# The first two column blocks of an output projection, computed as a pair

## The chip, the cores and the metric

The kernel runs on one core of a Trainium2 chip. Its engines work side by side: TensorE (PE in the profile, with PEld for the loads of stationary operands), VectorE (DVE), ScalarE (ACT), GpSimd (POOL) and SyncE (SP). The last two mostly issue DMA transfers here. The metric is device time in microseconds (us) of one execution, as the median of several runs.

## What is computed

One layer of a decoder trunk, on 256 rows of 2048 columns, in float32:

```python
def hybrid_layer(x, g_mix, w_in, q_gain, k_gain, w_branch, w_out, g_ffn, w_gu, w_down, rel_bias):
    h = rmsnorm(x, g_mix)
    proj = h @ w_in
...
    merged = (gates[:, :, 0] * (flat(o_a) @ w_branch[:ea])
              + gates[:, :, 1] * (flat(o_b) @ w_branch[ea:eb])
              + gates[:, :, 2] * (flat(o_c) @ w_branch[eb:]))
    x = x + merged @ w_out

    h2 = rmsnorm(x, g_ffn)
    gu = h2 @ w_gu
    x = x + (jax.nn.silu(gu[..., :D_FF]) * gu[..., D_FF:]) @ w_down
    return x
```

The change is in `merged @ w_out`: a 256 x 2048 matrix times a 2048 x 2048 one.

## The kernel before

**Products.** A float32 operand is split into a high and a low part (`split`, L107: a cast on ScalarE and a subtraction on VectorE), and a product of two operands is three matmuls into one accumulator: high by high, high by low, low by high (`product`, L169, with the matmuls on L172 to L174). The rows of the activations come in two halves of 128 (t = 0, 1), the 2048 columns of the inner dimension in 16 k-tiles of 128, and the output columns in blocks of 512. Weights are fetched from memory two k-tiles at a time (a tile of 128 x 1024 numbers, 4 KB a partition) and split by `parts` (L311) or `weights` (L122), which rotate through five buffers each of `w_hi` and `w_lo`.

**Plain blocks.** `project` (L147) computes one column block: for every k-tile, both halves, three matmuls.

**Pairs.** `project_pair` (L351) computes two column blocks A and B together. For the chunks of four k-tiles that are named in `acts.wc` it treats activations and weights as 2 x 2 blocks and makes the eight block products out of seven ("forms" 1 to 7), with sums of activations made beforehand (`sums`, L222; here `ms_sums`) and sums of weights made on the way: u = b11 + b12, then u + b22, then u + b21, and b12 + b22. Here b11 and b12 are the upper quarters of the chunk's weights for the two columns, b21 and b22 the lower ones. Chunks that are not in `acts.wc` are done plainly (`rest`, L366). `acts.wc` was (0, 1) throughout: two chunks by sevens, two plain. Four PSUM accumulators are used: X and Y (`banks()`, called ps or qs in turn) and Z and V (called z and v). On w_out and w_gu (`by_banks`, L348) form 1 is made in X and copied by ScalarE into Y (L376), form 5 in Z and copied into V (L378); form 2 then adds to Y, and the plain steps on column B add to V and Z. Later X is read out twice (`snapshot`, L326) while forms 6 and 7 are added to it. The results of column B (c12, c22) are ready before those of column A, and the callback `early` is called with them. `begin_pair` (L338) fetches and splits the first quarters of a pair; it is called at the end of the pair before, when that is told of the next one (`nxt`), or else at the start.

**Order.** A scheduler orders each engine's instructions by a simulated timeline, except those wrapped in `keep_in_program_order`, which keep the order of the code among themselves. The fetches of the pairs are so wrapped (`fetch`, L103); those of the plain blocks (L120) are not. Side work (transposes, norms, sums) is cut into steps, put in `stages`, and one step is taken at every weight tile.

**Memory.** `pool(..., "left")` puts pools on a stack that grows from one side. In the stage before, the stack held `pe0` (16 KB a partition, the sums of activations), `p1` (16 KB of raw attention output `o_raw` and 32 KB of the first stage's activations `h`) and `o` (32 KB, the attention output that the branch projections read). After the branch projections `p1` and `o` are closed, and `pe` (8 KB), `h2` (44 KB) and `gx` (six `g_raw` tiles and two `u` tiles of 4 KB) take their room from the bottom up, in the order in which they are made. A tile placed on room that was used before waits for the last reader of what lay there.

**The stage that is changed** (L976 to L1007) did column blocks 0 and 1 with `project`, one after the other, and blocks 3 and 2 as a pair. After each block `keep_x1` (L990) adds the residual x, stores the sum, and puts the normalisation and transposes of that block (`next_h`) into `stages`. Behind it come the pairs on w_gu, with `h2` as activations.

Of the kernel before, what the change touches and what calls it, by code (L numbers as in the profile page):

```python
# [1 line left out]

# [1 line left out]

# [18 lines left out]
KT = D // P  # L23
# [4 lines left out]
D_FF = 5632  # L28
NF = D_FF // P
NB = 512  # L30
# [25 lines left out]
def hybrid_block(ctx: ExitStack, tc: tile.TileContext, x, w_in, w_branch, w_out, w_gu, w_down, rel_bias,  # L56
                 onehot, extra, across, factors, out):
    nc = tc.nc
# [22 lines left out]
    def pool(stack, name, side, bufs=1):  # L81
        return stack.enter_context(tc.tile_pool(name=name, bufs=bufs, side=side, reuse_waits="tile"))

    h2_stack, ph1, pm, pgx = ExitStack(), ExitStack(), ExitStack(), ExitStack()
# [4 lines left out]
    gx = pool(pgx, "gx", "right", 2)  # L89
# [7 lines left out]
    def banks():  # L97

        turn.reverse()
        return [acc.tile([P, NB], F32, name=turn[1]) for _ in range(2)]  # L100
# [21 lines left out]
    def weights(w, row0, k0, nk, col0, there=()):  # L122

        for i, c in enumerate(range(k0, nk, 2)):
            raw = there[i] if i < len(there) else raw_weights(w, row0, c, col0)[0]
            hi = wpool.tile([P, 2, NB], F32R, name="w_hi")
            lo = wpool.tile([P, 2, NB], F32R, name="w_lo")
            split(hi, lo, raw)
            for k in range(2):
                yield c + k, hi[:, k, :], lo[:, k, :]  # L130
# [4 lines left out]
    def advance(queue):  # L135
        while queue:
            try:
                next(queue[0])
                return
            except StopIteration:  # L140
                queue.pop(0)
# [5 lines left out]
    def project(acts, k0, w, row0, nk, col0, ps=None, done=0, there=(), last=1):  # L147


        ps = ps or banks()  # L150
        held = []
        for k, w_hi, w_lo in weights(w, row0, done, nk, col0, there):
            if k:
                advance(stages)
            if k % 2 == 0 and k:
                advance(slow_stages)
            held.append((k, w_hi, w_lo))
            if k < nk - last or k == nk - 1:
                for t in range(NT):
                    for kk, hi, lo in held:  # L160
                        product(ps[t], *acts.plain(t, k0 + kk), hi, lo, kk == 0, kk == nk - 1)
                held = []
        return ps
# [5 lines left out]
    def product(ps, ah, al, wh, wl, start=False, stop=False):  # L169
        how = dict(skip_group_check=True)  # L170
        wh, wl = woven(wh), woven(wl)
        nc.tensor.matmul(ps, ah, wh, start=start, stop=False, **how)  # L172
        nc.tensor.matmul(ps, ah, wl, start=False, stop=False, **how)  # L173
        nc.tensor.matmul(ps, al, wh, start=False, stop=stop, **how)  # L174
# [60 lines left out]
    class Sums:  # L235
# [22 lines left out]
        def form(self, f, c, j):  # L258
# [2 lines left out]
                return [x[:, 2 * kh + j, t * P:(t + 1) * P] for x in self.s[c]]  # L261
            return self.plain(*{1: (0, 4 * c + j), 2: (0, 4 * c + 2 + j), 4: (1, 4 * c + 2 + j)}[f])

    class Chunks(Sums):


# [36 lines left out]
    WC = (0, 1)  # L303
# [7 lines left out]
    def parts(src):  # L311
        hi = wpool.tile([P, 2, NB], F32R, name="w_hi")
        lo = wpool.tile([P, 2, NB], F32R, name="w_lo")
        with tc.issue_after(fence.pop().ins) if fence else nullcontext():
            split_last[:] = split(hi, lo, src)
        advance(stages)
        split_count[0] += 1
        if split_count[0] % 2:
            advance(slow_stages)
        return hi, lo  # L320
# [5 lines left out]
    def snapshot(ps):  # L326
        sb = half_kb()
        nc.scalar.copy(sb, ps)  # L328
        return sb
# [18 lines left out]
    def by_banks(w):  # L348
        return w is w_gu or w is w_out

    def project_pair(acts, w, colA, colB, begun=None, nxt=None, by_dma=False, early=None):  # L351

        cols = (colA, colB)
        X, Y = banks()
        Z, V = others()

        def form(ps, f, srcs, start, stop, split=False):
            for i, c in enumerate(acts.wc):  # L360
                wh, wl = srcs[i] if split else parts(srcs[i])
                for j in range(2):
                    product(ps, *acts.form(f, c, j), wh[:, j], wl[:, j], start and i + j == 0,
                            stop and i + j == len(acts.wc))

        def rest(n, k, p0, p1, start=False, stop=False, raw=None):  # L366
            wh, wl = parts(raw or load(w, k, cols[n]))
            for t, ps in ((1, p1), (0, p0)):
                for j in range(2):
                    product(ps, *acts.plain(t, k + j), wh[:, j], wl[:, j], bool(start and t == 1 and j == 0), stop and j == 1)  # L370

        ks = [k for c in range(KT // 4) if c not in acts.wc for k in (4 * c, 4 * c + 2)]
        p11, b12, u, b21, second = begun or begin_pair(acts, w, colA, colB)
        form(X, 1, p11, True, True, True)
        if by_banks(w):
            tc.keep_in_program_order(nc.scalar.copy(Y, X))  # L376
            form(Z, 5, second, True, True, True)
            doubled[:] = [tc.keep_in_program_order(nc.scalar.copy(V, Z))]  # L378
            form(Y, 2, b21, False, False)
        else:  # L380
            s1 = snapshot(X)
            form(Y, 2, second, True, False, True)
            form(Z, 5, u, True, True)
            z5 = snapshot(Z)
        plain = [load(w, k, colB) for k in ks[:2]]
        b22 = quarter(acts, w, 1, colB)
        if by_dma:
            for d, a in zip(b12, b22):
                nc.gpsimd.dma_start(d, a, accum_op=ALU.add)  # L389
        rest(1, ks[0], Z, V, start=not by_banks(w), raw=plain[0])  # L390
        rest(1, ks[1], Z, V, raw=plain[1])
        add_into(u, b22)
        form(X, 6, u, False, True)
        for d, a in zip(u, b21):
            nc.gpsimd.dma_start(d, a, accum_op=ALU.add)  # L395
        x2 = snapshot(X)
        rest(1, ks[2], Z, V)
        if not by_dma:
            add_into(b12, b22)
        form(X, 7, b12, False, True)  # L400
        x3 = snapshot(X)
        rest(1, ks[3], Z, V, stop=True)
        c22 = half_kb()
        if by_banks(w):
            nc.vector.tensor_sub(c22, V, x3)
        else:
            nc.vector.tensor_sub(z5, z5, x3)
            nc.vector.tensor_add(c22, V, z5)
        form(Z, 3, b22, False, True)
        c12 = half_kb()  # L410
        nc.vector.tensor_sub(c12, Z, x2)
        if early:
            early(c12, c22)
        for k in ks[:2]:
            rest(0, k, Y, X)
        form(X, 4, u, False, False)
        for k in ks[2:]:
            rest(0, k, Y, X, stop=k == ks[-1])
        ahead = begin_pair(*nxt) if nxt else None
        if by_banks(w):  # L420
            return (Y, X, c12, c22), ahead
        c11 = half_kb()
        nc.vector.tensor_add(c11, Y, s1)
        return (c11, X, c12, c22), ahead
# [23 lines left out]
    def load_x(c, queue):  # L448
        xc = [half_kb() for _ in range(NT)]
        for t in range(NT):  # L450
            queue(xc[t], x[t * P:(t + 1) * P, c * NB:(c + 1) * NB])
        return xc
# [435 lines left out]
    ahead = None  # L888
    for (kind, what), after in zip(units, units[1:] + [(None, None)]):
# [9 lines left out]
        if kind in ("qk", "gates", "vv", "vg"):  # L899
            ps, ahead = project_pair(*pair_of(kind, what), ahead, nxt, others is in_turn)  # L900
            if others is in_turn:
                turn.reverse()
        else:
            ps = project(h, 0, w_in, 0, KT, V0 + what * NB if kind == "v" else gate_col(*what),
                         *((ps0, 4, there) if (kind, what) == ("v", 0) else ()))
            ahead = begin_pair(*nxt) if nxt else None
# [32 lines left out]
    m = Columns(pool(pm, "pm", "right"), "m", KT)  # L939

    ms_sums = Both(pe0, m, WC)
# [16 lines left out]
    for c in range(4):  # L958
        ms = [half_kb() for _ in range(NT)]
        for b, (k0, nk) in enumerate(((0, H_A), (H_A, H_B), (H_A + H_B, H_C))):  # L960
# [3 lines left out]
            ps = project(o, k0, w_branch, k0 * P, nk, c * NB)  # L964
# [9 lines left out]


    pe = pool(ctx, "pe", "left")  # L976
    h2 = Chunks(pool(h2_stack, "h2p", "left"), "h", KT // 4, WC)

    def next_h(c, xc):
# [10 lines left out]
    def keep_x1(c, ps, xc):  # L990
        for t in range(NT):
            nc.vector.tensor_add(xc[t], ps[t], xc[t])
            nc.gpsimd.dma_start(x1[t, :, c * NB:(c + 1) * NB], xc[t])
        squares(xc, ss2, c)
        stages.append(next_h(c, xc))

    gx = pool(h2_stack, "gx2", "left", 2)
    for c in range(2):
        xc = load_x(c, nc.gpsimd.dma_start)
        ps = project(m, 0, w_out, 0, KT, c * NB)  # L1000
        keep_x1(c, ps, xc)
    xs = {c: load_x(c, nc.gpsimd.dma_start) for c in (2, 3)}
    (c30, c31, _, _), ahead = project_pair(ms_sums, w_out, 3 * NB, 2 * NB, None, (h2, w_gu, 0, D_FF), True,
                                           lambda *c2: keep_x1(2, c2, xs[2]))
    doubled.clear()
    keep_x1(3, (c30, c31), xs[3])
# [304 lines left out]
```

## Time and profile before

| | |
|---|---|
| median of 3 runs | 1337.57 us (1337.1 to 1338.85) |
| the profiled execution | 1337.34 us |
| its span in the profile | 1335.6 us |
| matmuls on PE | 6243 |
| issues of w_out's weights | 24 into w_raw, 8 into g_raw, 512 KB each |

The profile shows one execution. Busy time of an engine is the time in which at least one of its instructions ran; a matmul's busy time overlaps that of the next, so the distance between their starts tells what one costs. "Idle before, releaser" names what ended a wait. A row of the timeline is: start, duration, engine, line, operation, output and inputs, count, and in brackets the idle time before it.

### The profile page before, as it was taken

Reading aid. Unit: us, or ns where it says so; the run is one execution under the profiler, and the core shown is the slowest. Engines: PE = TensorE matmul, PEld = TensorE weight load, DVE = VectorE, ACT = ScalarE, POOL = GpSimd, SP = SyncE. Lnnn points to the kernel's source line nnn. Section 1 sums busy time; section 2 is a strip of 40 time slices with the busy share of each in tenths; the row PEclk is TensorE's granted clock in tenths of the full one; section 3 lists DMA queues with packets and bytes.
Section 4 is the critical chain, followed back from the end, with each engine's and each line's share of the span. In section 5 each row is a group of like instructions: output and inputs, shape, how many; then the busy total and the mean of one; then the engine's idle time right before and its main releaser. Section 6 shows DMA issues by size and latency. Waiting matters only on the chain.

```text
span 1335.6 us, 17783 instructions
## 1 busy us (share of the span) xinstructions
PE 1328.6 (99%) x6243; PEld 1158.7 (87%) x6243; DVE 1168.9 (88%) x1254; ACT 940.9 (70%) x1209; POOL 130.9 (10%) x195
## 2 busy tenths in 40 slices
PE   9999999999999999999999999999999999999998
PEld 6888888888888888888888888888888888888887
DVE  7978898989888897986999999989899997998887
ACT  7786867788777776544777778777877875665563
POOL 1100110001111111100210000001000001001010
PEclk9999999999999999999999999999999999999999
DMA  9997878797788878877988889889899977789883
GB/s 359 308 282 246 263 210 258 252 277 223 263 267 282 277 241 289 294 249 244 305 312 267 259 265 278 238 252 308 279 286 274 281 216 253 252 276 301 270 271 96
DMA packets 119505, 354.70 MB, mean 266 GB/s; under 512 B 32832, under 2 KB 34552, under 8 KB 119416
## 3 DMA queue, kind: packets, MB, share of 16 engines
q1 hardware_dynamic: 77016, 277.45, 58.4%
q0 software_dynamic: 19984, 69.76, 22.2%
q10 hardware_dynamic: 22416, 6.36, 2.8%
q8 instruction: 49, 0.80, 0.2%
q14 instruction: 40, 0.33, 0.1%
HBM read 294.26 MB, written 14.70 MB: 231 GB/s over the span
## 4 chain that ended last, share of the span: by engine, by line
PE 98%; DMA 1%; ACT 0%; DVE 0%; SPq 0%; issue 0%; DVEq 0%
PE qs L172 12%; PE ps L173 12%; PE qs L174 12%; PE qs L173 12%; PE ps L174 12%; PE ps L172 12%; PE z L173 4%; PE z L172 4%; PE z L174 4%; PE v L172 2%; PE v L173 2%; PE v L174 2%; PE tr L174 1%; PE tr L172 1%; PE tr L173 1%; PE tr L205 1%
## 5 line engine op out<-in xcount | busy, mean ns | idle before, releaser
L108 DVE TENSOR_TENSOR w_lo<-w_raw,w_hi 128x1024 fp32r<-128x1024 f32 x302 | 366.0, 1220 | 57.9 <-ACT w_hi L108 56.6
L108 ACT CAST w_hi<-w_raw 128x1024 fp32r<-128x1024 f32 x302 | 313.7, 1047 | 111.3 <-PE qs L174 39.5
L108 ACT CAST w_hi<-g_raw 128x1024 fp32r<-128x1024 f32 x216 | 222.8, 1050 | 106.0 <-PE qs L174 32.9
L108 DVE TENSOR_TENSOR w_lo<-g_raw,w_hi 128x1024 fp32r<-128x1024 f32 x216 | 257.5, 1220 | 19.7 <-ACT w_hi L108 17.4
L108 ACT CAST w_hi<-u 128x1024 fp32r<-128x1024 f32 x162 | 168.7, 1049 | 107.1 <-PE qs L174 22.4
L108 DVE TENSOR_TENSOR w_lo<-u,w_hi 128x1024 fp32r<-128x1024 f32 x162 | 195.6, 1221 | 42.5 <-ACT w_hi L108 37.6
L173 PE MATMUL ps<-w_lo,h_hi 128*128 128x512 f32 x352 | 134.0, 381 | 0.5 <-DVE w_lo L108 0.5
L174 PE MATMUL ps<-w_hi,h_lo 128*128 128x512 f32 x352 | 133.5, 380 | 0.1
L172 PE MATMUL ps<-w_hi,h_hi 128*128 128x512 f32 x352 | 129.1, 382 | 0.0
L173 PE MATMUL qs<-w_lo,h_hi 128*128 128x512 f32 x332 | 126.5, 381 | 0.0
L174 PE MATMUL qs<-w_hi,h_lo 128*128 128x512 f32 x332 | 126.0, 380 | 0.0
L172 PE MATMUL qs<-w_hi,h_hi 128*128 128x512 f32 x332 | 121.3, 382 | 0.0
L173 PEld LDWEIGHTS ps<-w_lo,h_hi 128*128 128x128 f32 x352 | 66.5, 189 | 10.4 <-DVE w_lo L108 1.3
L174 PEld LDWEIGHTS ps<-w_hi,h_lo 128*128 128x128 f32 x352 | 66.5, 189 | 10.3 <-DVE h_lo L108 1.1
L395 POOL DMA_DIRECT2D u<-g_raw x46 | 40.1, 871 | 360.1 <-DVE w_lo L108 299.6
L172 PEld LDWEIGHTS ps<-w_hi,h_hi 128*128 128x128 f32 x352 | 66.3, 189 | 9.5 <-ACT h_hi L108 0.3
L172 PEld LDWEIGHTS qs<-w_hi,h_hi 128*128 128x128 f32 x332 | 62.7, 189 | 9.1 <-ACT sc L328 0.4
L173 PEld LDWEIGHTS qs<-w_lo,h_hi 128*128 128x128 f32 x332 | 62.8, 189 | 8.7
L174 PEld LDWEIGHTS qs<-w_hi,h_lo 128*128 128x128 f32 x332 | 62.8, 189 | 8.7
L344 DVE TENSOR_TENSOR u<-g_raw 128x1024 f32<-128x1024 f32 x46 | 56.0, 1219 | 13.1 <-DMA g_raw<-in_w_gu 9.5
L333 DVE TENSOR_TENSOR u<-u,g_raw 128x1024 f32<-128x1024 f32 x46 | 54.2, 1218 | 0.0
L389 POOL DMA_DIRECT2D g_raw<-g_raw x20 | 17.3, 867 | 252.2 <-DMA g_raw<-in_w_in 133.7
(440 smaller groups left out, 2977.2 us busy)
## 6 DMA issues: line engine op xcount, KB each, us to landing
w_raw<-in_w_in SPq DMA_DIRECT2D x103, 512.0 KB, 7.0
g_raw<-in_w_in SPq DMA_DIRECT2D x88, 512.0 KB, 6.2
g_raw<-in_w_gu SPq DMA_DIRECT2D x88, 512.0 KB, 6.2
w_raw<-in_w_gu SPq DMA_DIRECT2D x88, 512.0 KB, 6.4
w_raw<-in_w_down SPq DMA_DIRECT2D x56, 512.0 KB, 4.8
u<-g_raw POOLq DMA_DIRECT2D x50, 512.0 KB, 6.6
w_raw<-in_w_branch SPq DMA_DIRECT2D x32, 512.0 KB, 4.6
g_raw<-in_w_down SPq DMA_DIRECT2D x32, 512.0 KB, 5.0
```

What stands on the lines that cost most here:

```text
L108: cast, rest = nc.scalar.copy(hi, src), nc.vector.tensor_sub(lo, src, hi.bitcast(F32))
L172: nc.tensor.matmul(ps, ah, wh, start=start, stop=False, **how)
L173: nc.tensor.matmul(ps, ah, wl, start=False, stop=False, **how)
L174: nc.tensor.matmul(ps, al, wh, start=False, stop=stop, **how)
L205: nc.tensor.transpose(pt[:, i, :], src[:, i * P:(i + 1) * P], ident)
L333: tc.keep_in_program_order(nc.vector.tensor_add(d, d, a))
L344: nc.vector.tensor_add(d, a, b)
L389: nc.gpsimd.dma_start(d, a, accum_op=ALU.add)
L395: nc.gpsimd.dma_start(d, a, accum_op=ALU.add)
```

## The change

Blocks 1 and 0 of the output projection become a pair as well, with one chunk of four k-tiles (chunk 0) by sevens and the three others plain. `Sums.part` makes a view of the sums with fewer chunks. The plain steps on column B between form 7 and the end, one until now, become a loop, since there are now six plain steps and not four. The first pair is told of the second, which thus begins at its end. The pool `gx` is made before `h2`, so that it lies lower on the stack. The residual x of both blocks is loaded at the start.

```diff
+        def part(self, wc):
+
+            some = copy(self)
+            some.wc = wc
+            return some
...
-        rest(1, ks[3], Z, V, stop=True)
+        for k in ks[3:]:
+            rest(1, k, Z, V, stop=k == ks[-1])
...
     pe = pool(ctx, "pe", "left")
+    gx = pool(h2_stack, "gx2", "left", 2)
     h2 = Chunks(pool(h2_stack, "h2p", "left"), "h", KT // 4, WC)
...
-    gx = pool(h2_stack, "gx2", "left", 2)
-    for c in range(2):
-        xc = load_x(c, nc.gpsimd.dma_start)
-        ps = project(m, 0, w_out, 0, KT, c * NB)
-        keep_x1(c, ps, xc)
+    xs = {c: load_x(c, nc.gpsimd.dma_start) for c in (0, 1)}
+    (c10, c11, _, _), ahead = project_pair(ms_sums.part(WC[:1]), w_out, NB, 0, None, (ms_sums, w_out, 3 * NB, 2 * NB), True,
+                                           lambda *c2: keep_x1(0, c2, xs[0]))
+    keep_x1(1, (c10, c11), xs[1])
     xs = {c: load_x(c, nc.gpsimd.dma_start) for c in (2, 3)}
-    (c30, c31, _, _), ahead = project_pair(ms_sums, w_out, 3 * NB, 2 * NB, None, (h2, w_gu, 0, D_FF), True,
+    (c30, c31, _, _), ahead = project_pair(ms_sums, w_out, 3 * NB, 2 * NB, ahead, (h2, w_gu, 0, D_FF), True,
                                            lambda *c2: keep_x1(2, c2, xs[2]))
```

More of the change, by code (lines that the diff above doesn't have):

```diff
@@ L1 @@
 from contextlib import ExitStack, nullcontext
+from copy import copy
 import numpy as np
```

## The prediction

> **What bounds the kernel now.** I read the page first: busy shares, granted clock, chain.
>
> ```profile
> span 1335.6 us, 17783 instructions
> ...
> PE 1328.6 (99%) x6243; PEld 1158.7 (87%) x6243; DVE 1168.9 (88%) x1254; ACT 940.9 (70%) x1209; POOL 130.9 (10%) x195
> ...
> PEclk9999999999999999999999999999999999999999
> ...
> PE 98%; DMA 1%; ACT 0%; DVE 0%; SPq 0%; issue 0%; DVEq 0%
> ```
>
> TensorE is busy 99% of the span at full granted clock, and 98% of the chain that ended last is its own work. So the time is the number of matmuls times their pitch, plus TensorE's few waits. The list of who waits for whom, limited to PE, is short:
>
> ```profile
> PE tr L430 <- DVE sc L445: 1.1, 1, 1.1
> PE ps L533 <- ACT w_hi L527: 0.6, 1, 0.6
> PE ps L173 <- DVE w_lo L108: 0.5, 2, 0.2
> PE ps L536 <- DVE w_lo L530: 0.4, 1, 0.4
> ```
>
> Columns: total us, times, longest. Lines 430, 533 and 536 are the first stage, which stays as it is. Next the table by stretches for the output projection (us, then busy and count of PE, PEld, DVE, ACT, POOL; clock, DMA share, GB/s) and TensorE's timeline at its three borders:
>
> ```profile
> 600.00:622.00 22.00, 22.00 (x108) 19.32 (x107) 13.72 (x16) 9.47 (x10) 0.00 (x0) 1.00 0.64 207
> 622.00:643.00 21.00, 21.00 (x103) 18.46 (x102) 16.34 (x21) 11.50 (x16) 2.24 (x5) 1.00 0.90 310
> 643.00:683.00 40.00, 39.86 (x193) 34.73 (x192) 38.67 (x43) 30.30 (x46) 7.88 (x12) 1.00 0.98 316
> ```
>
> ```profile
> 600.13 0.38 PE L174 MATMUL ps<-w_hi,o_lo 128*128 128x512 f32 x1
> 600.35 0.38 PE L172 MATMUL qs<-w_hi,m_hi 128*128 128x512 f32 x1
> ...
> 606.17 1.04 PE L205 MATMUL tr<-ident,sc 128*128 128x128 f32 x8
> ...
> 643.54 0.38 PE L172 MATMUL qs<-w_hi,m_hi 128*128 128x512 f32 x1
> ...
> 684.54 0.38 PE L172 MATMUL ps<-w_hi,h_0hi 128*128 128x512 f32 x1
> ```
>
> The two plain blocks run from 600.35 to 643.54, the pair from there to 684.54. From 600.35 to the transposes at 606.17 are 27 matmuls: 5.82 / 27 = 0.2156 us each, while each one's busy time is 0.38, since they overlap. Two groups of eight transposes lie in the first stretch, and the chain gives one as
>
> ```profile
> 606.34 0.87 PE tr L205 x8
> ```
>
> So 43.19 - 2 x 0.87 = 41.45 us for 192 matmuls, 0.2159 us each. TensorE is full there; VectorE has 8.28 + 4.66 = 12.94 us free before 643, and only 1.33 of 40 after it.
>
> **Six matmuls fewer.** In a plain block one chunk of four k-tiles is 4 k-tiles x 2 row halves x 3 matmuls = 24, so 48 for two blocks. By sevens it is 7 forms x 2 k-tiles x 3 = 42. One chunk is done so: 6 x 0.2159 = **1.30 us** less on TensorE, all on the path (192 become 186). The page "TensorE: Matmul & The Clock Gate" of the Trainium skill, section "Back-to-back issue gap", gives about 131 ns a matmul for a sustained stream of weight loads and matmuls at 512 columns; six of these would be 0.79 us and the time some 1336.8. The same section's figure for an isolated matmul, about 216 ns, is what the rows above show.
>
> **What the pair needs first.** Form 1 needs chunk 0 of the merged activations, which is complete: 600.35 already multiplies it. The last chunk is first needed at ks[4], after 5 forms and 4 plain steps: 30 + 48 matmuls, 16.8 us into the stage. Plain block 0 reached it after 72 matmuls (15.5 us) and the same transposes, without a wait. Nothing is late there.
>
> **The weights.** The first pair's quarters no longer take w_raw buffers but the gx pool, now placed ahead of h2: after pe0 (16 KB a partition) and pe (8 KB) it takes six g_raw and two u of 4 KB, 32 KB. By the tile sizes in the code this lies within p1 (o_raw 16 KB, h 32 KB), not under o. The last reads of o_raw, the loads by SP's queue, and how long w_out's loads take:
>
> ```profile
> L108 DVE TENSOR_TENSOR o_lo<-o_raw,o_hi x4: 1211/1212/1215, 466.3 to 515.6; 128x1024 fp32r<-128x1024 f32 x4
> ...
> 560.63 18.39 SPq L120 DMA_DIRECT2D w_raw<-in_w_branch  x8
> 582.23 39.98 SPq L120 DMA_DIRECT2D w_raw<-in_w_out  x16
> 622.27 2.99 SPq L105 DMA_DIRECT2D g_raw<-in_w_out  x6
> ...
> DMA to landing us min/median/max: 3.3/4.7/14.1
> ```
>
> The room is free from 517 us on, and SP has issued its last w_branch load by 560.63 + 18.39 = 579.0. The first quarters can follow there: even the longest landing, 14.1, ends at 593, before TensorE turns to w_out at 600.35. The number of w_out loads stays 32 (12 g_raw and 20 w_raw for 8 and 24), all now through the pinned fetch. I cost the loads at nothing, covered by these 21 us. The same holds for the second pair: its six first quarters are queued behind the first pair's last w_raw, about as they were behind block 1's (622.27, for use at 643.54).
>
> **VectorE and ScalarE.** Added are three weight splits (19 for 16), two additions into u and the two subtractions for c12 and c22:
>
> ```profile
> L108 DVE TENSOR_TENSOR w_lo<-g_raw,w_hi 128x1024 fp32r<-128x1024 f32 x8 | 9.7, 1217 | 0.8 <-ACT w_hi L108 0.8
> ...
> L344 DVE TENSOR_TENSOR u<-g_raw 128x1024 f32<-128x1024 f32 x2 | 2.4, 1222 | 0.2 <-DVE w_lo L108 0.2
> ...
> L411 DVE TENSOR_TENSOR sc<-z,sc 128x512 f32<-128x512 f32 x1 | 0.7, 684 | 0.0
> ```
>
> That is 5 x 1.22 + 2 x 0.68 = 7.5 us of VectorE, against 12.94 - 1.30 = 11.6 free in its stretch. It would be about 90% busy; in the pair behind it 97% (38.67 of 40) went with one wait. ScalarE gets three casts and four copies, 3 x 1.05 + 4 x 0.6 = 5.6 us, where 22 of 43 are free. I cost both at nothing; if that cover goes, VectorE's work is late (third rival). Two accumulating DMAs are added on POOL, b22 into b12 and b21 into u; the like of the first in the pair now:
>
> ```profile
> 642.92 0.92 POOL L389 DMA_DIRECT2D g_raw<-g_raw  x1 [17.95 <-DMA g_raw<-in_w_out]
> ```
>
> POOL waits there 17.95 us for b22. Behind such a wait on POOL stand the x1 stores and the loads of x for the next blocks; x is needed only at the end of a block and x1 only in the last stage. The sum b12 is needed at form 7, 60 matmuls or 13 us into the stage, and b22, queued behind two plain loads (2.5 us each in the 582.23 row), can be there before 600: covered. x for both blocks is now held from the start, four of the twelve scratch tiles; no row shows a shortage of them, and I add nothing.
>
> **The copies that seed Y and V.** This is the one new wait on the path. A pair on w_out copies X to Y after form 1 and Z to V after form 5 by ScalarE, with the next form as cover. Two chunks make that cover 12 matmuls, one chunk 6, 1.30 us. In the pair now:
>
> ```profile
> 645.91 0.38 PE L174 MATMUL qs<-w_hi,m_lo 128*128 128x512 f32 x1
> ...
> 651.97 0.38 PE L174 MATMUL qs<-w_hi,m_lo 128*128 128x512 f32 x1
> 652.49 0.48 PE L172 MATMUL v<-w_hi,m_hi 128*128 128x512 f32 x1
> ```
>
> ```profile
> 647.39 0.57 ACT L376 COPY qs<-qs 128x512 f32<-128x512 f32 x1
> 647.90 1.99 ACT L108 CAST w_hi<-w_raw 128x1024 fp32r<-128x1024 f32 x2
> 649.80 2.14 ACT L460 ACTIVATE sc<-tr,fac 128x128 f32<-128x128 f32 x8
> 651.81 0.62 ACT L378 COPY v<-z 128x512 f32<-128x512 f32 x1
> ```
>
> Form 1 ends at 645.91 + 0.38 = 646.29 and the copy starts 1.10 later; the copy to V stood behind eight scalings (L460) and cost TensorE 652.49 - 651.97 - 0.22 = 0.30 us, with 0.09 more in the slower next matmul. With 6 matmuls of cover, 1.30 - (0.38 - 0.22) - 0.60 for the copy - 0.06 to the matmul leave 0.48 us by which ScalarE may be late. Bounds: nothing if ScalarE stands idle, as it does between casts at this place,
>
> ```profile
> 600.55 1.05 ACT L108 CAST w_hi<-w_raw 128x1024 fp32r<-128x1024 f32 x1 [1.54 <-PE ps L174]
> ```
>
> and 1.10 - 0.48 = 0.62 a copy, 1.24 for both, if each starts as late as the one above. I take 0.40 for the two, nearer to the idle row. The existing 0.39 may go: in the new order of the code the scalings of block 1 are queued behind the second pair's copies, not ahead of them; bounds 0 and -0.39, taken -0.20.
>
> **Sum**, against the profiled execution's own 1337.34 (span 1335.6 and 1.7 around it): -1.30 + 0.40 - 0.20 = -1.10, 1336.2. The median of the runs shown, 1337.57, stands 0.23 higher; I say **1336.3**.
>
> **Rivals.**
> 1. The seeds come late. Both copies at 1.24 and the old wait kept: 1337.34 - 1.30 + 1.24 = 1337.3. For it: pinned copies stand in order behind casts of 1.05. Against: ScalarE's 1.54 idle before each cast there. 13%.
> 2. The six cost less than the pitch, say no more than their weight loads (1158.7 / 6243 = 0.186 each): 1.11 saved, 1336.4. Against: PEld idles 13%, and starts lie 0.2156 apart wherever the timeline is read. The Trainium skill's 131 ns would be of this kind, with the 1336.8 above. 1%.
> 3. VectorE becomes the bound in the second pair; this ends slower. The order of all engines is made anew by the scheduler. What decides is how much of the 7.5 us lands behind the first pair's end, where only 1.33 are free and VectorE's lead is small:
>
> ```profile
> 654.47 1.22 DVE L108 TENSOR_TENSOR w_lo<-u,w_hi 128x1024 fp32r<-128x1024 f32 x1
> ...
> 657.77 0.38 PE L172 MATMUL qs<-w_hi,hi 128*128 128x512 f32 x1
> ```
>
> The split of form 6's first part ends at 655.69, 2.08 before TensorE uses it. So it costs from 1.33 + 2.08 = 3.4 us of shifted work on; if all 7.5 is shifted, 7.5 - 3.4 = 4.1, less 1.3 saved: 1340.1, and with the lead already eaten 1342.2. Against: the added work belongs to parts that TensorE needs before 641. 9%, of which 7 slower than the bound below.
> 4. The change doesn't do what it says of the room: a gx tile lies on o after all. Then no quarter can load before o's last matmul at 600.13: 0.4 to issue, 4.7 to land, 1.05 to cast, and 0.4 until the first product: 6.5 us of wait, 1342.6. Against: gx ends at 24 + 32 = 56 KB, p1 at 16 + 48 = 64. 4%.
> 5. More than 0.2% faster. No row has it: the saving and every wait behind 600 (0.39, and 0.2 on w_lo) make 1.9, and 2.7 are needed. Left for what a new order does elsewhere: 4%.
>
> **Numbers.** Forecast 69%. About 0.2%, 2.7 us, is what a measurement of this kernel can tell from no change. Faster by more: 4%. Slower by more: 7 + 4 = 11%. Within: 69 + 13 + 2 + 1 = 85%. Range: low end 1337.34 - 1.30 - 0.39 - 0.2 = 1335.4, and 0.4 for the scatter of runs: 1335.0. High end: the first rival at 1337.3, 0.23 for the median, and the lighter part of the third: 1338.6. Outside remain 4 + 4 and most of 9%.
>
> **What would show it.** 6237 matmuls on PE for 6243, 186 of them in the first pair where the two blocks had 192. The first pair from about 600.35 to 642.3, with 0.2159 between starts. The g_raw loads of w_out issued near 579; if near 600, rival 4. In the waits of PE, v or qs on ScalarE's L378 or L376 between 601 and 605 for rival 1, and w_lo on VectorE with DVE near 100% of 643 to 683 for rival 3. I am wrong if TensorE stands still for more than about 1 us between 600 and 725.

## The result, and the profile after

| | median | runs |
|---|---|---|
| before | 1337.34 us | 6 (1336.73 to 1338.93) |
| after | 1345.15 us | 6 (1343.78 to 1347.5) |

The changed kernel takes 1.0053 times as long (95% interval 1.0043 to 1.0063, which is 5.8 to 8.4 us): by the medians 7.8 us more, where 1.1 less were forecast. The profiled execution took 1347.5 us, its span is 1345.8. The page of the profile first:

```profile
span 1345.8 us, 17786 instructions
...
PE 1334.0 (99%) x6237; PEld 1159.7 (86%) x6237; DVE 1175.3 (87%) x1261; ACT 945.3 (70%) x1216; POOL 132.4 (10%) x197
...
PEclk9999999999999999998999999999999999999999
```

There are 6237 matmuls, six fewer, as meant. PE is still "99% busy", yet one slice of the granted clock shows 8. The slice is at the start of the first pair. The table by stretches of the changed kernel (us, then busy and count of PE, PEld, DVE, ACT, POOL; clock, DMA share, GB/s):

```profile
600.00:643.00 43.00, 39.58 (x167) 32.43 (x167) 31.80 (x32) 24.74 (x30) 2.93 (x4) 0.88 0.64 199
643.00:683.00 40.00, 40.00 (x191) 35.10 (x191) 38.91 (x48) 30.00 (x45) 7.36 (x11) 1.00 0.96 298
```

The first pair's stretch has 39.58 of 43 us busy at a clock of 0.88; before it was full at 1.00. The stretch behind it is full, with VectorE as busy as it was (38.91, before 38.67). So the loss is at the head of the first pair. TensorE's timeline there:

```profile
601.12 0.38 PE L175 MATMUL ps<-w_hi,o_lo 128*128 128x512 f32 x1
602.97 1.23 PE L206 MATMUL tr<-ident,sc 128*128 128x128 f32 x8 [1.47 <-DVE sc L978]
605.22 0.80 PE L173 MATMUL qs<-w_hi,m_hi 128*128 128x512 f32 x1 [1.02 <-ACT w_hi L109]
...
613.58 0.63 PE L173 MATMUL qs<-w_hi,m_hi 128*128 128x512 f32 x1
614.01 0.63 PE L174 MATMUL qs<-w_lo,m_hi 128*128 128x512 f32 x1
...
615.52 0.38 PE L175 MATMUL v<-w_hi,m_lo 128*128 128x512 f32 x1
615.73 0.38 PE L173 MATMUL v<-w_hi,m_hi 128*128 128x512 f32 x1
```

601.12 is the last matmul of the branch projections. Where the kernel before went on to w_out 0.22 later, TensorE now does the last eight transposes of the merged rows, after a wait, and its first product of the pair starts at 605.22. From 607.1 on, matmuls start 0.43 apart and not 0.216; at 615.52 the pitch (the distance between starts) is normal again. The profile grants half the clock just there, 0.50 from 605.07 to 615.30. Between 601.12 and 615.52 lie 21 matmuls and the transposes, which is 21 x 0.2159 + 0.87 = 5.4 us of work in 14.4: **9.0 us lost**, 5.1 as waits and 3.9 as slow pitch (9.04 from 606.48 to 615.52, less the 1.23 between 608.78 and 610.01, where TensorE waited for a low part, less 18 x 0.2159).

What TensorE waited for is in the chain that ended last:

```profile
601.28 0.23 PE ps L175
601.54 0.69 DVE sc L977
...
602.97 0.64 PE tr L206 x4
603.64 0.02 ACT m_hi L109
603.66 0.46 issue
604.12 1.06 ACT w_hi L109
...
605.20 1.23 DVE w_lo L109
606.43 1.14 DVE u L351
```

Read it as a relay with one runner at a time: last branch matmul, branch sums on VectorE, transposes, the rows' cast on ScalarE, and only then the cast of p11, the first weights of the pair (w_hi at 604.12), its low part, and the sum u, whose own cast and low part follow until 610. None of the weight steps needs anything of the branch. Were the weights not there? SP's queue and the landing of the three first quarters (the view by tile, 578 to 584):

```profile
580.06 1.90 SPq L106 DMA_DIRECT2D g_raw<-in_w_out  x3
...
DMA to landing us min/median/max: 6.8/8.9/10.3
```

They were: issued right behind the last w_branch load, landed by 581.3 (the start of the third issue) + 10.3 = 592. The two queues show why nobody used them. ScalarE in the changed kernel:

```profile
588.59 1.05 ACT L109 CAST w_hi<-w_raw 128x1024 fp32r<-128x1024 f32 x1 [1.30 <-PE qs L175]
603.64 0.58 ACT L109 CAST m_hi<-tr 128x512 fp32r<-128x512 f32 x1 [14.00 <-PE tr L206]
604.12 1.05 ACT L109 CAST w_hi<-g_raw 128x1024 fp32r<-128x1024 f32 x1
```

and VectorE:

```profile
600.89 1.34 DVE L977 TENSOR_TENSOR sc<-ps,sc 128x512 f32<-128x512 f32 x2 [5.23 <-PE ps L175]
602.14 1.28 DVE L978 TENSOR_TENSOR sc<-sc 128x512 f32<-128x512 f32 x2
604.25 0.69 DVE L109 TENSOR_TENSOR m_lo<-tr,m_hi 128x512 fp32r<-128x512 f32 x1 [0.82 <-ACT m_hi L109]
605.20 1.23 DVE L109 TENSOR_TENSOR w_lo<-g_raw,w_hi 128x1024 fp32r<-128x1024 f32 x1 [0.26 <-ACT w_hi L109]
```

On VectorE the branch products and sums (L977, L978) stand ahead of p11's low part. ScalarE stands idle for 14 us in front of a cast of transposed rows that cannot start, with the cast of p11 queued behind it. In the kernel before, ScalarE at the same place cast w_out's tiles one after the other:

```profile
590.19 1.05 ACT L108 CAST w_hi<-w_raw 128x1024 fp32r<-128x1024 f32 x1 [1.54 <-PE qs L174]
...
605.73 1.05 ACT L108 CAST w_hi<-w_raw 128x1024 fp32r<-128x1024 f32 x1 [1.54 <-PE qs L174]
606.81 1.07 ACT L108 CAST m_hi<-tr 128x512 fp32r<-128x512 f32 x2
```

Later in the changed kernel TensorE loses 0.8 us on low parts at 707 and 712, where it lost 0.2 before, and the old wait of 0.39 at 652 is gone. These sum to 9.0 - 1.30 - 0.39 + 0.6 = 7.9, beside 7.8 between the medians. But they are read from one execution, the slowest of the six, which took 10.2 us more than the profiled one before. The rest of these 10.2 is 1.0 in the first stage, which the change leaves as it is (the last branch matmul starts at 601.12 for 600.13), and 1.4 in short waits between 806 and 831. No run shows whether the change has a part in these, nor how the other five executions divide.

**Theory T**: each engine serves its queue in order, and in the changed kernel the first splits of the pair stand behind work that waits for the last branch matmul; the idle time then halves the clock for a while. **Rivals**: the room or the loads cost it, the seeds or VectorE do, or the pair's own chain of cast, low part, sum and cast.

### The profile page after: what moved, and what is told of

Its sections match the earlier page's. It is cut to its first block, busy times and chain, and to the rows that moved or that the text cites. A ratio compares the mean times of both kernels' runs of the same rounds, so it can differ in the third digit from the quotient of the medians.

```text
span 1345.8 us, 17786 instructions
## 1 busy us (share of the span) xinstructions
PE 1334.0 (99%) x6237; PEld 1159.7 (86%) x6237; DVE 1175.3 (87%) x1261; ACT 945.3 (70%) x1216; POOL 132.4 (10%) x197
## 4 chain that ended last, share of the span: by engine, by line
PE 96%; DVE 1%; DMA 1%; ACT 0%; issue 0%; SPq 0%; DVEq 0%; ACTq 0%
PE qs L174 12%; PE qs L173 12%; PE qs L175 12%; PE ps L174 11%; PE ps L175 11%; PE ps L173 11%; PE z L174 4%; PE z L175 4%; PE z L173 4%; PE v L173 3%; PE v L175 3%; PE v L174 3%; PE tr L175 1%; PE tr L174 1%; PE tr L173 1%; PE tr L206 1%
## 5 line engine op out<-in xcount | busy, mean ns | idle before, releaser
L109 DVE TENSOR_TENSOR w_lo<-w_raw,w_hi 128x1024 fp32r<-128x1024 f32 x298 | 360.8, 1218 | 50.2 <-ACT w_hi L109 48.8
L109 ACT CAST w_hi<-w_raw 128x1024 fp32r<-128x1024 f32 x298 | 309.2, 1047 | 97.8 <-PE qs L175 28.1
L109 ACT CAST w_hi<-g_raw 128x1024 fp32r<-128x1024 f32 x220 | 226.7, 1050 | 101.6 <-DVE g_raw L340 31.5
L109 DVE TENSOR_TENSOR w_lo<-g_raw,w_hi 128x1024 fp32r<-128x1024 f32 x220 | 262.2, 1219 | 21.2 <-ACT w_hi L109 18.8
L174 PE MATMUL qs<-w_lo,h_hi 128*128 128x512 f32 x348 | 132.8, 382 | 0.0
L175 PE MATMUL qs<-w_hi,h_lo 128*128 128x512 f32 x348 | 132.1, 379 | 0.0
L174 PE MATMUL ps<-w_lo,h_hi 128*128 128x512 f32 x336 | 128.0, 381 | 0.4 <-DVE w_lo L109 0.4
L175 PE MATMUL ps<-w_hi,h_lo 128*128 128x512 f32 x336 | 127.4, 380 | 0.1
L173 PE MATMUL qs<-w_hi,h_hi 128*128 128x512 f32 x348 | 127.4, 382 | 0.0
L173 PE MATMUL ps<-w_hi,h_hi 128*128 128x512 f32 x336 | 123.0, 382 | 0.0
```

Of the source, the lines that this page charges most:

```text
L109: cast, rest = nc.scalar.copy(hi, src), nc.vector.tensor_sub(lo, src, hi.bitcast(F32))
```

## The experiments

Each kernel was timed beside the kernel before; the ratio is to it, and its median in that comparison stands beside.

| kernel | median | before | ratio (95%) |
|---|---|---|---|
| e1_room_alone | 1338.03 | 1338.0 | 1.0002 (0.9994 to 1.0011) |
| e2_old_room | 1345.71 | 1338.0 | 1.0054 (1.0041 to 1.0067) |
| e3_kept_busy | 1344.3 | 1338.0 | 1.0042 (1.0027 to 1.0056) |
| e4_splits_first | 1345.03 | 1338.0 | 1.0060 (1.0039 to 1.0080) |
| e6_sums_too | 1336.64 | 1338.19 | 0.9994 (0.9983 to 1.0005) |
| e7_third_too | 1343.38 | 1338.19 | 1.0039 (1.0026 to 1.0051) |
| e8_two_chunks | 1342.71 | 1338.19 | 1.0032 (1.0021 to 1.0043) |
| e9_late_splits | 1345.17 | 1338.19 | 1.0049 (1.0035 to 1.0062) |
| e6_again | 1336.55 | 1337.62 | 0.9996 (0.9987 to 1.0004) |
| e10_two_chunks | 1335.41 | 1337.62 | 0.9980 (0.9971 to 0.9988) |
| e11_late_rows | 1335.63 | 1337.62 | 0.9994 (0.9979 to 1.0009) |
| e12_sums_old_room | 1346.2 | 1337.62 | 1.0062 (1.0049 to 1.0075) |

**e1_room_alone**: the kernel before, with the pool moved.

```diff
     pe = pool(ctx, "pe", "left")
+    gx = pool(h2_stack, "gx2", "left", 2)
     h2 = Chunks(pool(h2_stack, "h2p", "left"), "h", KT // 4, WC)
...
-    gx = pool(h2_stack, "gx2", "left", 2)
```

> The kernel before with only the room moved: the three buffers gx2 are made ahead of h2, and blocks 0 and 1 stay plain. Theory T (the loss lies in the order of ScalarE's and VectorE's queues where the first pair begins): nothing of this is here, so the time of the kernel before, 1337.3 within 0.2% (1334.7 to 1340.0), and no idle time of TensorE over 1 us between 600 and 620. Rival R (giving the room early costs something by itself, a load or a buffer that comes later elsewhere): well over the kernel before, up to 1345.

No difference: 1.0002. The move of the room costs nothing.

**e2_old_room**: the changed kernel, with the pool moved back (the same two lines the other way round).

> The changed kernel with gx2 back in its old place in the code, so that it lies on room that o holds to its last matmul; the order of the instructions on ScalarE and TensorE stays as in the changed kernel. Theory T: the room did what it should, so without it the three loads of the first quarters wait for the last matmul of the branch at about 601, land 3.4 to 8.2 us later, and the first cast of p11, now at 604.1, comes at about 609.5; 4 to 7 us over the changed kernel's 1345.1, that is 1349 to 1352. If the loads play no part: 1345, as the changed kernel.

Measured 1345.71, as the changed kernel, so this expectation of T failed. SP's queue of e2, the landing of the three loads (by tile, 600 to 602), and ScalarE:

```profile
600.30 1.28 SPq L106 DMA_DIRECT2D g_raw<-in_w_out  x3
...
DMA to landing us min/median/max: 3.7/4.6/5.4
```

```profile
602.62 0.59 ACT L109 CAST m_hi<-tr 128x512 fp32r<-128x512 f32 x1 [14.00 <-PE tr L206]
604.04 1.05 ACT L109 CAST w_hi<-g_raw 128x1024 fp32r<-128x1024 f32 x1 [0.83 <-DMA g_raw<-in_w_out]
```

The loads did wait, for 20 us. But with nothing else on the way (DMA share 0.00 from 590 to 600) the first landed in 3.7 us, and its cast, again behind the rows' cast, waited 0.83 for it. What follows is stronger than what was expected: with this order of the queues it makes almost no difference whether the weights come at 592 or at 604. The order hides the gain of the early room.

**e9_late_splits**: the kernel before with nothing of the change but its order. Two splits of plain block 0 are pinned behind the rows' casts.

```diff
-            split(hi, lo, raw)
+            split(hi, lo, raw, w is w_out and col0 == 0 and i < 2)
```

> The kernel before, all blocks as they were, with only the first two splits of the weights of block 0 (k-tiles 0 to 3) pinned behind the splits of the last merged rows on ScalarE and VectorE, which puts the last eight transposes ahead of the block's first matmul on TensorE. No room, load, seed or sum of the change is in it. Theory T: the same idle time as in the changed kernel, transposes at about 603, first product at about 605, clock down to about half for some 10 us: 5 to 9 us over the kernel before, 1342.5 to 1346.5. Rival (the loss comes from the pair's own chain or room): within 1 us of the kernel before.

Measured 1345.17, 7.0 over the kernel before. TensorE's timeline of e9, and ScalarE's row at this place:

```profile
600.12 0.38 PE L174 MATMUL ps<-w_hi,o_lo 128*128 128x512 f32 x1
601.98 1.23 PE L205 MATMUL tr<-ident,sc 128*128 128x128 f32 x8 [1.48 <-DVE sc L970]
604.82 1.22 PE L172 MATMUL qs<-w_hi,m_hi 128*128 128x512 f32 x2 [1.62 <-ACT w_hi L108]
...
606.67 0.63 PE L174 MATMUL qs<-w_hi,m_lo 128*128 128x512 f32 x1
```

```profile
602.64 1.19 ACT L108 CAST m_hi<-tr 128x512 fp32r<-128x512 f32 x2 [14.00 <-PE tr L205]
```

The same picture as in the changed kernel: ScalarE idle for the same 14.00 us, TensorE idle for 1.48 and 1.62 us (there 1.47 and 1.02), then the slow pitch, without room, pair, seeds or sums. The order alone is enough for the loss. One part of the expectation missed: the clock was at half for 3.4 us and not for some 10, in an execution that was the fastest of its four (1343.2).

**e4_splits_first** and **e6_sums_too**: the order undone in the changed kernel. In e4, `begin_pair` is written ahead of the steps of the last merged rows, and these rows' transposes and splits are pinned behind it. e6 also writes the last four branch operations behind it:

```diff
-    finish_stages(stages)
+    held, stages[:] = stages[:], []
...
+    begun = begin_pair(ms_sums.part(WC[:1]), w_out, NB, 0)
+    for t in range(NT):
+        tc.keep_in_program_order(nc.vector.tensor_mul(gt[t], ps[t], gt[t]))
+    for t in range(NT):
+        tc.keep_in_program_order(nc.vector.tensor_add(ms[t], ms[t], gt[t]))
+    stages[:] = held
```

(The two loops over t in e6 alone; in e4 these operations stay where they were.)

> The changed kernel with one thing moved: the first sums and splits of the pair (p11 and its neighbour) are written ahead of the splits of the last merged rows on ScalarE and VectorE, and the pair's first two forms ahead of the last eight transposes on TensorE. Theory T (the loads were there by 592, but the splits stood behind casts that wait for the transposes): ScalarE casts the first quarter before 600, TensorE never stands still over 1 us between 600 and 620, clock 1.00, and the time is 1336.0 to 1336.5, 1 us under the kernel before as the count of matmuls has it. Rival R1 (the quarters themselves come too late): 1343 or more, with the idle time still ahead of p11. Rival R2 (the seeds' copies or VectorE are the cost): 1337.3 to 1342, with waits on them between 604 and 683.

> The changed kernel with the first sums and splits of the pair ahead of the last merged rows on both engines: on ScalarE as in e4_splits_first, and now on VectorE too, where the last four branch operations (two products, two sums, 2.6 us) stand behind the splits of p11 and of u. Theory T, mended (both queues are served in order, and e4 freed only ScalarE's: VectorE's low parts of p11 and u still stood behind the branch operations, which wait for the last branch matmul): both splits are done before 600, forms 1 and 5 run on from the last branch matmul without a gap, the clock stays at 1.00, at most 1.5 us of idle time is left behind them, where VectorE catches up; 1336.0 to 1337.5 beside 1337.5 of the kernel before. Rival R1 (something else than the order holds the head of the pair, the quarters' landing or the chain cast, low part, sum, cast): 1342 or more, with TensorE still idle for over 3 us between 600 and 616. Rival R2 (the seeds' copies or VectorE in the second pair): 1338 to 1342 with the waits between 604 and 725.

> The kernel of e6_sums_too once more, to narrow its interval: by the count of matmuls 1.30 us and the old wait of 0.39 us under the kernel before, so 0.9988 to 0.9993 of it; if the first result was chance, 1.000 or above.

e4 changed nothing in the time, 1345.03: the second expectation of T that failed. (Its profiled execution took 1354.28, the other five 1343.39 to 1346.77; only the head is read from it.) ScalarE and VectorE:

```profile
592.17 1.05 ACT L109 CAST w_hi<-g_raw 128x1024 fp32r<-128x1024 f32 x1 [1.54 <-PE qs L175]
606.81 1.04 ACT L109 CAST w_hi<-u 128x1024 fp32r<-128x1024 f32 x1 [13.59 <-DVE u L353]
```

```profile
601.89 1.34 DVE L979 TENSOR_TENSOR sc<-ps,sc 128x512 f32<-128x512 f32 x2 [5.23 <-PE ps L175]
...
604.34 1.22 DVE L109 TENSOR_TENSOR w_lo<-g_raw,w_hi 128x1024 fp32r<-128x1024 f32 x1
```

The cast of p11 is now done at 593, 12 us earlier. Its low part is not: it stands on VectorE behind the branch operations (L979, L980), so TensorE waits 2.90 for it, and the chain through u is as late as ever. Half an order freed is nothing gained. (e4 already has the pair's first two forms ahead of the transposes on TensorE, so it is not TensorE's own order that counts.) In e6 both queues are free, and VectorE shows it:

```profile
594.45 1.22 DVE L109 TENSOR_TENSOR w_lo<-g_raw,w_hi 128x1024 fp32r<-128x1024 f32 x1
595.59 1.22 DVE L353 TENSOR_TENSOR u<-g_raw 128x1024 f32<-128x1024 f32 x1
598.00 1.23 DVE L109 TENSOR_TENSOR w_lo<-u,w_hi 128x1024 fp32r<-128x1024 f32 x1 [1.19 <-ACT w_hi L109]
599.77 1.34 DVE L1011 TENSOR_TENSOR sc<-ps,sc 128x512 f32<-128x512 f32 x2 [0.55 <-PE ps L175]
```

and its table by stretches:

```profile
600.00:643.00 43.00, 43.00 (x209) 37.78 (x208) 37.90 (x43) 26.39 (x34) 3.46 (x5) 1.00 0.78 264
643.00:683.00 40.00, 40.00 (x195) 35.16 (x194) 39.25 (x45) 31.30 (x49) 6.52 (x11) 1.00 0.94 299
```

TensorE is full in both stretches at a clock of 1.00. 1336.64 and 1336.55, in the two comparisons 1.55 and 1.07 under the kernel before, and 8 to 9 under the changed kernel. That is about the 1.1 that the prediction had for the whole change, though neither interval excludes 1.

**e12_sums_old_room**: e6 with the room back under o.

> e6_sums_too with the three buffers gx2 back on the room that o holds; the order of the instructions on ScalarE, VectorE and TensorE up to the second pair stays. Theory T says that the room alone buys nothing while the splits stand late (e2) and is needed once they stand early: the loads are issued at about 600.3, land at about 604, TensorE is idle from 601 to about 605 and again for the sum's chain, clock down; 5 to 9 us over e6, 1341 to 1346. If the room does not matter: as e6, 1336.6.

1346.2, 9.6 over e6 in the same comparison, a little more than expected. ScalarE now stands 15.35 us ahead of the cast of p11 for the load, and TensorE 4.58 for the cast. With the splits early, the early room is what carries them.

**e3_kept_busy**: how much of the loss is the clock. The changed kernel with 11 extra matmuls in the idle time, whose output nothing reads.

```diff
+    def busy(n):
+
+        nothing = tr.tile([P, NB], F32, name="tr")
+        for _ in range(n):
+            tc.keep_in_program_order(nc.tensor.matmul(nothing, m.hi[:, 0, 0:P], m.hi[:, 0:2, :], start=True, stop=True))
...
+    busy(6)
     finish_stages(stages)
+    busy(5)
```

> The changed kernel with 11 extra matmuls of 512 columns in TensorE's idle time, 6 just ahead of the last eight transposes of the merged rows and 5 just behind them; nothing reads what they write, and the order of all other instructions is that of the changed kernel. They add no work beside the idle stretches (11 x 0.216 = 2.4 us, and TensorE is idle for 2.9 us there). Theory T with the clock as part of the cost (about 20 matmuls at 0.43 apart for 0.216, 4.2 us): the granted clock stays at 1.00, the pitch at 0.216, and the time is about 4 us under the changed kernel, 1341. If the waits alone count, or the slow pitch has another cause (operands that come late): 1345, or up to 1346 if the extra matmuls push the transposes.

TensorE's timeline of e3:

```profile
606.80 0.38 PE L173 MATMUL qs<-w_hi,m_hi 128*128 128x512 f32 x1
607.01 0.38 PE L174 MATMUL qs<-w_lo,m_hi 128*128 128x512 f32 x1
...
608.53 0.48 PE L173 MATMUL z<-w_hi,hi 128*128 128x512 f32 x1 [0.92 <-ACT w_hi L109]
609.79 0.48 PE L174 MATMUL z<-w_lo,hi 128*128 128x512 f32 x1 [0.78 <-DVE w_lo L109]
```

The clock stays at 1.00 from 600 to 615.5 (0.67 in the changed kernel) and the pitch at 0.216. Counted as above, the extra matmuls as lost time, the head loses 6.6 us for 9.0, so 2.4 are won where 4 were expected: the faster matmuls arrive sooner at form 5 (z) and wait there for u's cast, 1.08, and low part, 1.04 (from start to start, less one pitch), where the slow ones waited for the second alone. In the medians it is 6.3 over the kernel before, where the change was 7.8 (1341 was expected, 1344.3 measured); the intervals overlap, so the total alone would not show it.

**e7_third_too, e8_two_chunks, e10_two_chunks, e11_late_rows**: can the saving be made larger? e7 also splits the third quarter early; e8 adds the second chunk by sevens to e7. e10 adds the second chunk to e6, and e11 puts the rows' steps four splits later in e10.

```diff
+    begun += ([parts(b) for b in begun[3]],)
...
-            form(Y, 2, b21, False, False)
+            form(Y, 2, third[0] if third else b21, False, False, bool(third))
```

```diff
-    begun = begin_pair(ms_sums.part(WC[:1]), w_out, NB, 0)
+    begun = begin_pair(ms_sums, w_out, NB, 0)
...
-    stages[:] = held
+    stages[:] = [iter(range(4))] + held
```

(The first diff is e7's against e6. The upper half of the second, with the same edit in the call of `project_pair`, makes e8 of e7 and e10 of e6; the lower makes e11 of e10.)

> e6_sums_too with the split of the third quarter (b21) ahead of the last branch operations as well, so that forms 1, 5 and 2 (18 matmuls, 3.9 us) stand ready. Theory T: what e6 leaves of idle time where VectorE catches up goes to under 1 us; 1336.0 to 1336.8. If e6 leaves none, the same as e6. If the room of five split buffers is what holds (the fifth is taken by the last branch weights): a wait before 600 in place of one behind it, and the same time as e6 or more.

> e7_third_too with two chunks of four k-tiles by sevens in the first pair, as the second pair has them: six matmuls fewer (1.30 us by the pitch of 0.216), two more sums and two more adds by DMA. Theory T: TensorE stays the bound, 1334.7 to 1335.5. Rival: VectorE becomes the bound in the first pair (its work there is 31.8 of 43 us in the changed kernel): 1337 or more, with waits on the low parts between 610 and 643.

> e6_sums_too with two chunks of four k-tiles by sevens in the first pair (six matmuls fewer again, 1.30 us). On ScalarE the casts of the last merged rows stand ahead of the casts of form 6's sums, as in e7_third_too. Theory T: no wait in the head; where the rows' casts stand ahead of form 6's, the transposes come 24 matmuls earlier on TensorE than the wait in e7 did, so at most 1.5 us of idle time; 1335 to 1337. Rival (what held e7 and e8 is the order in which ScalarE takes the rows' casts and the sums' casts, and it is still there): 2 to 5 us idle ahead of form 6 between 610 and 620, 1339 to 1343.

> e10_two_chunks with the last merged rows' transposes and splits four splits later, behind the casts of form 6's sums on ScalarE. If the order of these casts is what held e7 and e8: no idle time over 1 us between 600 and 643, 1334.7 to 1335.8, unless VectorE or the transposes' way to k-tiles 12 to 15 is now late (a wait on the low part of the rows just ahead of them, 1 to 3 us). If VectorE bounds the first pair: as e10.

e7 lost 6.7 us to e6, and e8 6.1: two more expectations of T that failed. About 4 us of e7's loss come of the same mechanism at another place; the rest are later waits, 0.66 at 654 for a copy on ScalarE and 0.92 and 0.29 at 703 and 709 for low parts. ScalarE of e7, and the matmul that waits:

```profile
609.05 0.59 ACT L109 CAST m_hi<-tr 128x512 fp32r<-128x512 f32 x1 [4.03 <-PE tr L206]
611.00 0.59 ACT L109 CAST m_hi<-tr 128x512 fp32r<-128x512 f32 x1 [1.36 <-PE tr L206]
613.53 1.04 ACT L109 CAST w_hi<-u 128x1024 fp32r<-128x1024 f32 x1 [1.95 <-DVE u L342]
```

```profile
614.63 0.48 PE L173 MATMUL qs<-w_hi,hi 128*128 128x512 f32 x1 [3.02 <-ACT w_hi L109]
```

The cast of form 6's sum stands behind the rows' casts, and the sum itself on VectorE behind their low parts; TensorE waits 3.02 for it. e8 shows the same wait, 3.66, and the slow pitch behind it. In e10, with the rows' casts ahead of form 6 as well, the two groups of transposes stand 27 and 22 matmuls ahead of form 6 on TensorE (in e7 10 and 3, in e8 10 and 0), and no wait is left between 600 and 683: 1335.41, as expected, and **0.9980 (0.9971 to 0.9988) of the kernel before**, the lowest median of all. Its table by stretches:

```profile
600.00:643.00 43.00, 43.00 (x209) 37.73 (x208) 40.98 (x44) 29.85 (x37) 5.56 (x7) 1.00 0.93 287
```

VectorE is now at 40.98 of 43, and at 39.97 of 40 behind it, and still no bound. In e11 TensorE is as full there; its median is 0.2 over e10's, and its interval is too wide to tell them apart. So the order of the rows' and the sums' casts alone decides nothing; by these traces it costs where the transposes are late too. (e7 and e10 differ in more than that, so this is read and not isolated.)

## Why the prediction was wrong

- **What bounds the kernel** was right. TensorE is the bound, and e6 and e10 gain what the matmuls saved are worth: e10's second six bring 1.14 over e6 in the same comparison (1.30 by the pitch). Rival 2 is out: starts lie 0.216 apart in e6 as before.
- **The weights**: the room, the issue at 579 (580.06 measured) and the landing before 593 were right, and so the fourth rival's mechanism did not occur. "I cost the loads at nothing, covered by these 21 us" is true of the loads and says nothing of the first product.
- **The step that failed** is "I cost both at nothing" for VectorE and ScalarE. It weighed 7.5 us of work against 11.6 us of free time, as if free time were a place where work can go. The queues are served in order: 14 us of ScalarE's free time stood in front of the one cast that TensorE needed. e9 shows that this order alone costs 7.0, e4 that freeing one of the two queues gains nothing, e6 that freeing both gains it all back. The only loss that the prediction saw in the new order of all engines was work shifted behind the first pair's end; the place that mattered was the first pair's start.
- **"Nothing is late there"**, said of what the pair needs first, looked at chunk 0 of the activations and at when TensorE needs the last rows. It did not ask what is queued ahead of p11's split on each engine.
- **The clock** was not thought of: 3.9 of the 9.0 us, of which e3 won back 2.4. That "TensorE stands still" would be a sign of error was written down, but not that such waits can be paid again in the matmuls behind them.
- **The seeds** were over-priced: 0.40, where e6 has no wait of TensorE between 600 and 683, so 0. The old wait of 0.39 went whole, not half. Rival 1 is out, and so is rival 3: VectorE is 39.25 of 40 us busy behind the pair in e6 without a wait. The 0.6 at 707 and 712 in the changed kernel is all that looks like it.
- **The fourth rival's price**, 6.5 us if the room lay on o, was the right kind of sum, with the clock left out: e12 against e6 gives 9.6, the clock included. In the changed kernel's own order it would have cost nearly nothing (e2).

Why the scheduler chose this order stays open; no run of its own tried it. What fits: a split from a gx tile is placed by when the scheduler expects that tile, and e2, where the tiles do come 20 us later, has the same order of ScalarE and TensorE as the changed kernel, as if early room made no difference to it.

## What to carry to other kernels

Free time of an engine covers a new step only if nothing ahead of that step in the engine's queue waits for the very work that is to be covered: list what stands ahead of the first step on each engine of its chain, cast and subtraction both. When a move brings a load forward, check that its consumers moved too. And price a stall of TensorE above its own length, since the matmuls behind it can run at half the clock.

## What the runs showed of the hardware

Between 601.5 and 605.2 TensorE of the changed kernel did eight transposes only, with 1.47 us of idle time ahead of them and 1.02 behind; the granted clock is 0.50 from 605.07 to 615.30, and the pitch 0.43 us, twice the normal. The Trainium skill, "TensorE: Matmul & The Clock Gate", section "What's actually happening", has the array at half clock after about one idle window of 3.4 us, the windows running free of the program. The 0.50 and the 0.43 agree with half clock; but TensorE was not idle for 3.4 us on end here, so less than that was enough.

How long it lasts does not follow from the idle time. In e9 nearly the same waits (1.48 and 1.62) were followed by 3.41 us at 0.50 (604.69 to 608.10), in e2 waits of 1.48 and 1.95 by 3.41 (606.43 to 609.84), in the changed kernel by 10.23. e3's waits of 0.80, 0.92 and 0.78 with short bursts between them brought none, and neither did e7's single one of 3.02. Even one kernel varies: e2's mean clock is 0.999 in the profiled execution and 0.996 in the other three. What the stretches have in common is their unit: 3.41 in e2 and e9, twice that in e4 (608.10 to 614.93), e8 (617.79 to 624.61) and e12 (602.82 to 609.64), and three times in the changed kernel. A clock that is set anew every 3.41 us would give this; no run shows more than that it fits.
